# Modulation steps of a two-layer diffusion backbone, placed by hand around its layer norms

## The chip, the core and the metric

The kernel runs on one core of one Trainium2 chip. Its engines are TensorE (PE for the matmul, PEld for its weight load), VectorE (DVE), ScalarE (ACT), GpSimd (POOL) and SyncE (SP), which here only issues DMA transfers. The metric is the device time of one execution in microseconds; lower is better.

## The reference, cut to what matters

Two layers work on 384 tokens of width 1024: 128 context tokens (tile 0) and 256 latent tokens (tiles 1 and 2). A small matrix product on two conditioning vectors, `c_ctx` and `c`, gives each layer its six modulation vectors (shift, scale and gate, for each of the two sub-layers):

```python
mod = silu(c) @ ada_w[l] + ada_b[l]                    # ada_w[l] is 1024 x 6144
shift1, scale1, gate1, shift2, scale2, gate2 = split(mod, 6)
mix = mixing_sublayer(x * (1 + scale1) + shift1)       # mLSTM, convolution, retention, merged by gates
x = layer_norm(ALPHA * x + gate1 * mix, ln1_w, ln1_b)
h = x * (1 + scale2) + shift2
a, gt = split(h @ ffn_w13, 2)                          # 1024 x 5632
x = layer_norm(ALPHA * x + gate2 * ((silu(gt) * a) @ ffn_w2), ln2_w, ln2_b)
```

All is float32. The outputs are the tokens and the final states of the context's scans.

## The kernel before, in words

**Matmuls.** A float32 product is made of three fast ones: activations and weights are each split into a high and a low part (`whl`, `split`, L205 on ACT and L206 on DVE), and `accum` (L255 to L257) adds high x high, high x low and low x high in PSUM. `colsA` makes channel-major results, all 384 tokens at a time; `tokB` makes token-major ones, one tile of 128 tokens and 512 channels at a time, which is 24 matmuls for a depth of 1024. `wrows` and `wcols` load weights in pieces of up to 1 MB into three buffers (wraw, L211 and L243), all issued from SP's queue.

**Modulation steps.** A layer's modulation is cut into three blocks of 2048 columns. `ada_steps` (L356) turns one block into nine closures: eight each load 1 MB of `ada_w` into wada (L369; one buffer, `WADA = 1`) and run four short matmuls into one PSUM bank (L371; eight records each); the first also loads the bias, the eighth adds it on DVE (L375) and sends the gates out through POOL's queue (L381); the ninth transposes the rows (L387) and copies them to `modT`. Layer 0's first block is computed ahead of everything. The other five, 45 closures, lie in the list `fillers`; `fill()` (L153) runs the next one. They have due times: the norm after layer 0's mixing needs the first two blocks, the norm after its FFN the third, and the loops at L1077 and L1097 run what is missing by then.

**Where they run.** `tick()` (L161) is called after each group of matmuls. It adds `rate["fill"]`, 0.3, to a counter, and at each whole number it runs one step. So there is a step behind every third or fourth group, wherever that falls, until the list is empty.

**The norms.** `proj` (L453) multiplies by an output weight in two halves of 512 channels, three token tiles each, and adds the gated result to the residual x (`resid`, L423 to L431). In the last half `norm` follows per tile: the statistics on DVE (L436, L318), the power -0.5 on POOL (L319), the normalisation on DVE (L442). Then `after(t)` runs `make_hT`: eight transposes of x on PE (L306), scale and shift on ACT (L310), the split into high and low on DVE (L313, L314), so that h2 (or h1 of the next layer) is there for the next projection; and `affine` on POOL (L450, L451), which brings x itself up to date. `after` is held back by one tile: tile 0's transposes come behind tile 1's matmuls, tile 1's behind tile 2's, and tile 2's in the middle of the second tile of the next projection (`lead`, the parameter `mid` of `tokB`). The next projection is `ffn_in` (L887; its first 512 columns go by `tokB`) after the mixing, and the value projections of layer 1 (L1110 to L1114) after layer 0's FFN. After layer 1's FFN comes the output; there is no `after`.

**Order.** The kernel is written in the Tile framework. The framework puts each engine's instructions in order by its own model of when each is ready, with the program's order as the priority; so an engine's order can differ from the program's.

Of the kernel before, what the change touches and what calls it, by code (L numbers as in the profile page):

```python
# [35 lines left out]
WADA = 1  # L36
TAPS1, TAPS2 = 2.0, 4.5
FILL = 0.3
LEADN = 4
AORD = {(0, 0): ((1, 1, 0, 16),), (0, 1): ((0, 1),), (0, 4): ((1, 2, 0, 16),), (0, 5): ((0, 2),),  # L40
        (1, 3): ((1, 3, 0, 16),), (1, 5): ((0, 3),)}
# [4 lines left out]
O_MQ, O_MK, O_MV, O_MO, O_MG = 0, 512, 1024, 1536, 2048  # L46
# [51 lines left out]
def tile_kernel(ctx: ExitStack, tc: tile.TileContext, a: dict, o: list):  # L98
# [17 lines left out]
    def psum(name="ps"):  # L116
        return pp.tile([P, 512], F32, tag="ps", name=name)
# [4 lines left out]
    def tmp(shape, tag, bufs=2, dt=F32):  # L122
        n = 1
        for v in shape[1:]:
            n *= v
        if n in NB and bufs != 1:
            return sm.tile(list(shape), dt, tag=f"w{n}", name=tag, bufs=NB[n])
        return sm.tile(list(shape), dt, tag=tag, name=tag, bufs=bufs)
# [7 lines left out]
    rate = {"fill": 0.0, "acc": 0.0, "taps": 0.0, "tacc": 0.0}  # L136
# [16 lines left out]
    def fill(n=1):  # L153
        for _ in range(min(n, len(fillers))):
            fillers.pop(0)()
# [68 lines left out]
    def wrows(src, nk):  # L224

        out = []
        for k0 in range(0, nk, 4):
            n = min(4, nk - k0)
            raw = wraw(src[k0 * P:(k0 + n) * P, :], n)
            for k in range(0, n, 2):  # L230
                hi, lo = whl([P, 2, 512], raw[:, k:k + 2, :])
                out += [(hi[:, i, :], lo[:, i, :]) for i in range(2)]
        return out
# [17 lines left out]
    def accum(out, pairs, first=True, last=True):  # L251

        n = len(pairs)
        for i, ((sh, sl), (vh, vl)) in enumerate(pairs):
            mm(out, sh, vh, start=(first and i == 0), stop=False)  # L255
            mm(out, sh, vl, start=False, stop=False)  # L256
            mm(out, sl, vh, start=False, stop=(last and i == n - 1))  # L257
# [27 lines left out]
    def tokB(ha, w, t, mid=None):  # L285

        ps = psum()
        s = slice(t * P, (t + 1) * P)
        pairs = [(ha.part(k, s), w[k]) for k in range(len(w))]
        if mid is None:  # L290
            accum(ps, pairs)
        else:
            n = len(w) * LEADN // 8
            accum(ps, pairs[:n], True, False)
            mid()
            accum(ps, pairs[n:], False, True)
        return ps
# [96 lines left out]
    def mod_affine(shift, scale, w, b):  # L394

        S = tmp((P, KT, 2), "modS")
        ts_(S, scale, 1.0, None, op0=ALU.add)
        B = tmp((P, KT, 2), "modB")
        for m in range(2):
            tt(B[:, :, m], S[:, :, m], b, op=ALU.mult)  # L400
            tt(B[:, :, m], B[:, :, m], shift[:, :, m], op=ALU.add)
            tt(S[:, :, m], S[:, :, m], w, op=ALU.mult)
        return S, B
# [49 lines left out]
    def proj(src, w, lc, first, final=False, after=None):  # L453


        nk = w.shape[0] // P
        late = []
        for hf in range(2):
            wl = wrows(w[:, hf * 512:(hf + 1) * 512], nk)
            for t in range(NT):  # L460
                ps = tokB(src, wl, t)
                resid(t, hf, ps, lc, first, final)
                if final and hf == 1:
                    norm(t, lc if after is None else None)
                    if after is None:
                        put_out(t)
                    else:
                        late.append(t)
                        if len(late) > 1:
                            after(late.pop(0))  # L470
                tick()
        return lambda: [after(t) for t in late]

    def put_out(t):
        for hf in range(2):
            s = slice(hf * 512, (hf + 1) * 512)
            if t == 0:
                nc.sync.dma_start(y_prompt[0, :, s], x[0][:, s])
            else:
                nc.sync.dma_start(y_sample[0, (t - 1) * P:t * P, s], x[t][:, s])  # L480

    def pv(l, v, n):
        return pvec[:, l, v:v + n]


    def put_v(dst, e):
        return lambda ps, t: nc.scalar.copy(dst[:, t, :, 0:e], ps.rearrange("p (h e) -> p h e", e=e))

    def alloc_v():
        v1 = sm.tile([P, NT, NH, 129], F32, tag="v1", name="v1", bufs=1)  # L490
        nc.gpsimd.memset(v1[:, :, :, 128:129], 1.0)
        return v1
# [394 lines left out]
    def ffn_in(l, h2, k0, n, lead=None):  # L887

        fA = Act(n, "fA")
        w = a["ffn_w13"][l]  # L890
        c0 = k0 * P
        if lead is not None:
            sgB = []
            wl = wrows(w[:, FF + c0:FF + c0 + 512], KT)
            for t in range(NT):
                ps = tokB(h2, wl, t, lead if t == NT - 2 else None)
                s_ = tmp((P, 512), "sgB")
                act(s_, ps, AF.Silu)
                sgB.append(s_)
                tick()  # L900
            wl = wrows(w[:, c0:c0 + 512], KT)

            def turn(t):
                ps = psum()
                for j in range(4):
                    tr(ps[:, j * P:(j + 1) * P], sgB[t][:, j * P:(j + 1) * P], ident)  # L906
                fA.put4(0, t, ps.rearrange("p (j c) -> p j c", c=P))

            for t in range(NT):
                ps = tokB(h2, wl, t)  # L910
                tt(sgB[t], ps, sgB[t], op=ALU.mult)
                if t:
                    turn(t - 1)
                tick()
            late = [lambda: turn(NT - 1)]
            c0 += 512
        else:
            late = []
        for c1 in range(c0, (k0 + n) * P, 256):
            sg = {}  # L920

            def put_g(ps, j):
                sg[j] = tmp((P, T), "sig")
                act(sg[j], ps, AF.Silu)

            def put_a(ps, j):
                f = tmp((P, T), "gf")
                tt(f, ps, sg[j], op=ALU.mult)  # L928
                fA.put(j, f)

            colsA(w[:, FF + c1:FF + c1 + 256], 256, h2, KT, put_g, c1 // P - k0)
            for f in late:
                f()
            late = []
            colsA(w[:, c1:c1 + 256], 256, h2, KT, put_a, c1 // P - k0)
        return fA
# [136 lines left out]
    fillers += ada_steps(0, 1) + ada_steps(0, 2) + ada_steps(1, 0) + ada_steps(1, 1) + ada_steps(1, 2)  # L1073
    rate["fill"] = FILL
    for l in range(DEPTH):
        mA = mixing(l, ha, v1, rv)
        while l == 0 and len(fillers) > 27:  # L1077
            fill()
        S2, B2 = mod_affine(modT[l][:, 1, 8:16, :], modT[l][:, 2, 0:8, :], pv(l, V_L1W, 8), pv(l, V_L1B, 8))
        h2 = Act(KT, "h2")  # L1080
        lc = ln_consts(l, 0)

        def after1(t):
            make_hT(h2, t, S2, B2)
            affine(t, lc)

        lead = proj(mA, a["out_w"][l], lc, True, True, after1)
        lc2 = None
        for k0, n in ((0, 8), (8, 6), (14, 8)):
            fA = ffn_in(l, h2, k0, n, lead if k0 == 0 else None)  # L1090
            if lc2 is None:
                lc2 = ln_consts(l, 1)
            w2 = a["ffn_w2"][l, k0 * P:(k0 + n) * P, :]
            if k0 + n < KF:
                proj(fA, w2, lc2, k0 == 0)
            elif l + 1 < DEPTH:
                while len(fillers) > 18:  # L1097
                    fill()
                S1, B1 = mod_affine(modT[l + 1][:, 0, 0:8, :], modT[l + 1][:, 0, 8:16, :],
                                    pv(l, V_L2W, 8), pv(l, V_L2B, 8))  # L1100
                ha = Act(KT, "h1")

                def after2(t):
                    make_hT(ha, t, S1, B1)
                    affine(t, lc2)

                lead2 = proj(fA, w2, lc2, False, True, after2)
                v1 = alloc_v()
                rv = m6((P, NT, NH, P), name="rv")
                for off, dst in ((O_MV, v1), (O_RV, rv)):  # L1110
                    wl = wrows(a["in_w"][l + 1][:, off:off + 512], KT)
                    for t in range(NT):
                        put_v(dst, P)(tokB(ha, wl, t, lead2 if t == NT - 2 and off == O_MV else None), t)
                        tick()  # L1114
            else:
                proj(fA, w2, lc2, False, True)
# [28 lines left out]
```

## Time and profile before

| | |
|---|---|
| median of 3 runs | 1488.73 us (1486.75 to 1489.26) |
| profiled execution, its own time | 1490.92 us |
| its span | 1488.9 us |
| mean granted clock of PE | 0.984 of full speed |
| HBM read | 221.18 MB |

A page of the profile tells what each engine did in one execution. "Busy" is time in which an instruction ran. PE's matmuls overlap, so their durations add up to more than the time they take; the distance between starts is what one costs. In a timeline each row has the start in us from the start of the span, the length in us, the engine, the line of the kernel, the operation, result <- inputs, shape, count, and in brackets the engine's idle time before it with what ended it. Names are the program's: ps and adaps are PSUM banks, whi and wlo the halves of a weight, h1h, h1l, h2h and h2l those of an activation.

### The profile page before, as it was taken

The numbers are of one execution on the slowest core, as the hardware profiler recorded it, in microseconds if no ns is written. First come the engines' busy times: TensorE is split into PE (matmuls) and PEld (weight loads), VectorE is DVE, ScalarE is ACT, GpSimd is POOL, SyncE is SP. The second block draws the span as 40 slices with busy tenths as digits, with TensorE's granted clock in tenths as the row PEclk, the third lists the DMA queues.
The fourth block names the chain that finished last, engine by engine and source line by source line (L and its number), as shares of the span: only waits on it lengthen the run. The fifth ranks groups of instructions, "written<-read, shape, count | busy, mean of one in ns | idle before, by whom it ended". The sixth has DMA issues, their size and how long they took to land. (4 is left out here: it accounts for less than half of the span.)

```text
span 1488.9 us, 20492 instructions
## 1 busy us (share of the span) xinstructions
PE 1438.7 (97%) x7990; PEld 1302.5 (87%) x7990; DVE 944.7 (63%) x1755; ACT 576.8 (39%) x1026; POOL 233.2 (16%) x242
## 2 busy tenths in 40 slices
PE   6999999999998999999999999989999989999997
PEld 4799999989986888979967999989999869899996
DVE  3457688996647545354375477989975674454446
ACT  2434555332523423323243345553325243242330
POOL 1003233002214100000042023320021250000000
PEclk8999999999999999999999999999999999999999
DMA  9465352464473474645644532324434525243441
GB/s 330 159 226 173 125 185 87 154 226 158 138 259 128 142 254 131 222 155 173 212 141 122 162 118 81 118 68 124 132 108 147 169 71 202 82 155 100 142 156 42
DMA packets 131713, 226.22 MB, mean 152 GB/s; under 512 B 12552, under 2 KB 62200, under 8 KB 126496
## 3 DMA queue, kind: packets, MB, share of 16 engines
q1 hardware_dynamic: 130144, 222.78, 45.2%
q0 software_dynamic: 1472, 2.14, 0.5%
q8 instruction: 62, 1.02, 0.3%
q14 instruction: 35, 0.29, 0.1%
HBM read 221.18 MB, written 3.71 MB: 151 GB/s over the span
## 5 line engine op out<-in xcount | busy, mean ns | idle before, releaser
L205 ACT CAST whi<-wraw 128x512 fp32r<-128x512 f32 (+1 forms) x484 | 338.7, 722 | 624.5 <-PE ps L256 268.1
L206 DVE TENSOR_TENSOR wlo<-wraw,whi 128x512 fp32r<-128x512 f32 (+1 forms) x484 | 403.5, 857 | 195.4 <-PE ps L257 92.4
L255 PE MATMUL ps<-h1h,whi 128*128 128x384 f32 x896 | 306.0, 341 | 0.0
L257 PE MATMUL ps<-h1h,wlo 128*128 128x384 f32 x896 | 299.9, 335 | 0.0
L256 PE MATMUL ps<-h1l,whi 128*128 128x384 f32 x896 | 299.8, 335 | 0.0
L255 PE MATMUL ps<-h2h,whi 128*128 128x384 f32 x576 | 193.9, 337 | 0.0
L257 PE MATMUL ps<-h2h,wlo 128*128 128x384 f32 x576 | 192.6, 334 | 0.0
L256 PE MATMUL ps<-h2l,whi 128*128 128x384 f32 x576 | 192.6, 334 | 0.0
L255 PEld LDWEIGHTS ps<-h1h,whi 128*128 128x128 f32 x896 | 168.4, 188 | 13.7 <-issue 8.4
L256 PEld LDWEIGHTS ps<-h1l,whi 128*128 128x128 f32 x896 | 168.5, 188 | 0.1
L257 PEld LDWEIGHTS ps<-h1h,wlo 128*128 128x128 f32 x896 | 168.3, 188 | 0.0
L756 DVE SCALAR_TENSOR_TENSOR cacc<-u,cwt,cacc 128x399 f32<-128x399 f32 x232 | 148.6, 661 | 2.0
L255 PEld LDWEIGHTS ps<-h2h,whi 128*128 128x128 f32 x576 | 108.1, 188 | 8.5 <-issue 4.2
L256 PEld LDWEIGHTS ps<-h2l,whi 128*128 128x128 f32 x576 | 108.1, 188 | 0.2
L257 PEld LDWEIGHTS ps<-h2h,wlo 128*128 128x128 f32 x576 | 108.1, 188 | 0.0
L255 PE MATMUL ps<-whi,fAh 128*128 128x512 f32 x264 | 103.4, 392 | 0.0
L257 PE MATMUL ps<-whi,fAl 128*128 128x512 f32 x264 | 102.9, 390 | 0.0
L256 PE MATMUL ps<-wlo,fAh 128*128 128x512 f32 x264 | 102.8, 389 | 0.0
L423 DVE TENSOR_TENSOR gmix<-ps,lnc 128x512 f32<-128x512 f32 x48 | 33.1, 689 | 81.2 <-PE ps L257 81.2
L928 DVE TENSOR_TENSOR gf<-ps,sig 128x384 f32<-128x384 f32 x36 | 20.1, 558 | 91.1 <-PE ps L257 91.1
L319 POOL TENSOR_TENSOR rs<-rs_ve,half 128x1 f32<-128x1 f32 x18 | 15.4, 856 | 380.8 <-DVE rs_ve L318 380.8
L844 POOL TENSOR_TENSOR mg<-mg,sig 128x384 f32<-128x384 f32 x32 | 42.4, 1330 | 200.5 <-DVE sig L843 200.5
(303 smaller groups left out, 2194.8 us busy)
## 6 DMA issues: line engine op xcount, KB each, us to landing
wraw<-in_in_w_dram SPq DMA_DIRECT2D x64, 1024.0 KB
wada<-in_ada_w_dram SPq DMA_DIRECT2D x40, 1024.0 KB
wraw<-in_ffn_w_dram SPq DMA_DIRECT2D x76, 512.0 KB
wraw<-in_ffn_w_dram SPq DMA_DIRECT2D x28, 1024.0 KB
wraw<-in_out_w_dram SPq DMA_DIRECT2D x8, 1024.0 KB
adaq<-in_ada_w_dram SPq DMA_DIRECT2D x8, 512.0 KB
wraw<-in_mlstm_out_w_dram SPq DMA_DIRECT2D x4, 1024.0 KB
wraw<-in_ret_out_w_dram SPq DMA_DIRECT2D x4, 1024.0 KB
```

The lines of the kernel that those rows point to most:

```text
L205: nc.scalar.copy(hi, src)
L206: tt(lo, src, hi.bitcast(F32), op=ALU.subtract)
L255: mm(out, sh, vh, start=(first and i == 0), stop=False)
L256: mm(out, sh, vl, start=False, stop=False)
L257: mm(out, sl, vh, start=False, stop=(last and i == n - 1))
L319: nc.gpsimd.tensor_tensor(out, ve, half[:, 0:shape[1]], op=ALU.pow)
L423: tt(g, ps, lc[0 if t == 0 else 1, hf], op=ALU.mult)
L756: stt(ac, u[:, k:k + CW], wk, ac, op0=ALU.mult, op1=ALU.add)
L844: nc.gpsimd.tensor_tensor(dst, dst, sg[j], op=ALU.add)
L928: tt(f, ps, sg[j], op=ALU.mult)
```

## The change

Three places get a call of `fill()`: in `proj`, ahead of each `after(t)` (the one that is left for later is now a function that fills first); in `ffn_in`, ahead of the second token tile of the first projection; and ahead of the second token tile of layer 1's first value projection. The rate of the counter is lowered from 0.3 to 0.1 from the end of layer 0's mixing until the end of its FFN, and to 0.0 in layer 1's; between them 0.3 holds again.

```diff
+FILLS = (0.1, 0.0)
...
                     else:
                         late.append(t)
                         if len(late) > 1:
+                            fill()
                             after(late.pop(0))
                 tick()
-        return lambda: [after(t) for t in late]
+        def rest():
+            fill()
+            for t in late:
+                after(t)
+
+        return rest
...
             for t in range(NT):
+                if t == 1:
+                    fill()
                 ps = tokB(h2, wl, t, lead if t == NT - 2 else None)
...
             fill()
+        rate["fill"] = FILLS[l]
         S2, B2 = mod_affine(modT[l][:, 1, 8:16, :], modT[l][:, 2, 0:8, :], pv(l, V_L1W, 8), pv(l, V_L1B, 8))
...
                 lead2 = proj(fA, w2, lc2, False, True, after2)
+                rate["fill"] = FILL
                 v1 = alloc_v()
                 rv = m6((P, NT, NH, P), name="rv")
                 for off, dst in ((O_MV, v1), (O_RV, rv)):
                     wl = wrows(a["in_w"][l + 1][:, off:off + 512], KT)
                     for t in range(NT):
+                        if t == 1 and off == O_MV:
+                            fill()
                         put_v(dst, P)(tokB(ha, wl, t, lead2 if t == NT - 2 and off == O_MV else None), t)
                         tick()
```

## Rows read from the trace of the kernel before

**Rows 1.** The page, part 1: busy time, share of the span, instructions.
```profile
PE 1438.7 (97%) x7990; PEld 1302.5 (87%) x7990; DVE 944.7 (63%) x1755; ACT 576.8 (39%) x1026; POOL 233.2 (16%) x242
```

**Rows 2.** PE's timeline, first norm: start, length, instruction, idle before.
```profile
458.90 1.03 PE L306 MATMUL ps<-cc,x 128*128 128x128 f32 x8
...
459.87 1.07 PE L371 MATMUL adaps<-wada,cs 128*32 128x512 f32 x8
...
467.83 1.11 PE L306 MATMUL ps<-cc,x 128*128 128x128 f32 x8 [1.22 <-DVE x L442]
...
476.83 0.50 PE L255 MATMUL ps<-whi,h2h 128*128 128x512 f32 x1 [1.68 <-DVE h2h L313]
...
478.52 0.80 PE L257 MATMUL ps<-whi,h2l 128*128 128x512 f32 x1 [0.95 <-DVE h2l L314]
...
482.95 1.85 PE L306 MATMUL ps<-cc,x 128*128 128x128 f32 x8
...
487.50 1.06 PE L371 MATMUL adaps<-wada,cs 128*32 128x512 f32 x8
...
488.49 0.50 PE L255 MATMUL ps<-whi,h2h 128*128 128x512 f32 x1
```

**Rows 3.** Windows: busy time by engine, granted clock, DMA share, GB/s.
```profile
465.00:466.00 1.00, 1.00 (x7) 0.81 (x5) 1.00 (x1) 0.68 (x2) 1.00 (x2) 1.00 0.20 82
...
784.00:786.00 2.00, 2.00 (x6) 1.52 (x5) 1.56 (x5) 0.00 (x0) 0.99 (x1) 0.50 0.62 185
```

**Rows 4.** POOL's timeline, first norm.
```profile
459.58 2.98 POOL L450 TENSOR_TENSOR x<-x,lnc 128x512 f32<-128x512 f32 x2 [2.65 <-PE ps L306]
...
465.67 1.53 POOL L319 TENSOR_TENSOR rs<-rs_ve,half 128x1 f32<-128x1 f32 x1
```

**Rows 5.** PE's timeline, second norm and first norm of layer 1.
```profile
773.03 1.11 PE L306 MATMUL ps<-cc,x 128*128 128x128 f32 x8 [1.22 <-DVE x L442]
...
782.02 0.79 PE L255 MATMUL ps<-whi,h1h 128*128 128x512 f32 x1 [1.67 <-DVE h1h L313]
...
1188.72 1.03 PE L306 MATMUL ps<-cc,x 128*128 128x128 f32 x8
...
1197.64 1.67 PE L306 MATMUL ps<-cc,x 128*128 128x128 f32 x8 [2.40 <-DVE x L442]
```

**Rows 6.** PE's timeline, both ends of the FFN body of layers 0 and 1.
```profile
504.96 0.60 PE L906 MATMUL ps<-cc,sgB 128*128 128x128 f32 x4
...
735.62 0.39 PE L255 MATMUL ps<-whi,fAh 128*128 128x512 f32 x1
...
1233.99 0.60 PE L906 MATMUL ps<-cc,sgB 128*128 128x128 f32 x4
...
1447.85 0.39 PE L255 MATMUL ps<-whi,fAh 128*128 128x512 f32 x1
```

**Rows 7.** DVE's timeline, first norm.
```profile
464.55 2.24 DVE L206 TENSOR_TENSOR wlo<-wraw,whi 128x1024 fp32r<-128x1024 f32 x1
...
486.94 1.65 DVE L314 TENSOR_TENSOR h2l<-hf,h2h 128x512 fp32r<-128x512 f32 x1
```

**Rows 8.** Instructions that touch tile x: durations ns min/median/max, first, last.
```profile
L425 DVE SCALAR_TENSOR_TENSOR x<-x,gmix x24: 691/693/1774, 436.8 to 1308.2; 128x512 f32<-128x512 f32 x24
```

**Rows 9.** SP's timeline: DMA issues, three stretches.
```profile
294.43 0.97 SPq L243 DMA_DIRECT2D wraw<-in_in_w_dram  x2
...
296.87 0.34 SPq L369 DMA_DIRECT2D wada<-in_ada_w_dram  x1
...
461.00 0.34 SPq L369 DMA_DIRECT2D wada<-in_ada_w_dram  x1
...
774.93 0.37 SPq L211 DMA_DIRECT2D wraw<-in_in_w_dram  x1
...
778.89 0.37 SPq L243 DMA_DIRECT2D wraw<-in_in_w_dram  x1
```

**Rows 10.** PE's timeline, a step in layer 0's branches.
```profile
309.68 1.15 PE L371 MATMUL adaps<-wada,cs 128*32 128x512 f32 x8 [2.24 <-DMA wada<-in_ada_w_dram]
```

## The prediction

> **What bounds the kernel now.** I read the page's busy times first: PE is busy for 1438.7 us, 97% of the span [rows 1]. A PE step that is moved from one full stretch to another therefore changes nothing; it gains only where PE would have stood still. So I looked next at where PE stands still, in PE's timeline around the first norm of layer 0, line 1087 [rows 2]. The reader is to see three sets of transposes (L306, one per token tile: 458.90, 467.83, 482.95) and waits behind them: 1.22 us before the second set, then 1.68 and 0.95 us in the first half of the second token tile of the next projection. From 478.52 on the clock is low too: that matmul takes 0.80 us, the transposes at 482.95 take 1.85 instead of 1.03, and in the windows view the same place of the second norm, 784 to 786, has a granted clock of 0.50, so 1.2 GHz instead of 2.4 [rows 3].
>
> Then I asked who makes PE wait, in POOL's timeline [rows 4]. The first transposes release POOL's affine work on that tile (459.58); it lasts until 465.67, where POOL takes the next tile's L319 at once, and only behind that can DVE normalise (L442) and PE transpose. From transposes to transposes that is 467.83 - 458.90 = 8.93 us. In layer 1, where no step stands between, it is 1197.64 - 1188.72 = 8.92 us [rows 5]. The norm's chain sets this distance, not PE's work. The second norm of layer 0 has nearly the same waits, 1.22 and 1.67 us [rows 5].
>
> **The change, part by part.** *What moves.* There are 45 steps (40 with a 1 MB wada load and short matmuls, 5 that close a block), before and after. Following the counter in `tick` through the code: up to line 1087 nothing changes. In the FFN body of layer 0 (first L906 to the last projection) 15 steps become 5; in layer 1's mixing 3 become 8. Between the first transposes and the third tile of the next projection there were 2 steps in each of layer 0's two norms; now there are 4: one ahead of each set of transposes, one ahead of the second tile. One stays ahead of each stretch, in another place, and one more comes after the second. In layer 1's norms nothing is left to run, so `FILLS[1]` and the calls do nothing there.
>
> *What a step costs in a full stretch.* Layer 0's FFN body, with 15 steps, takes 735.62 - 504.96 = 230.66 us; layer 1's, without any, 1447.85 - 1233.99 = 213.86 [rows 6]. So 16.8 / 15 = 1.12 us each, and one step on PE's timeline is 1.07 us [rows 2]. Four steps leave full stretches: 4 x 1.12 = -4.5 us. The five that go to layer 1's mixing I cost like any other, nothing hides them: no gain, no loss.
>
> *What they cost in the norm.* I walk the first norm with old times from [rows 2] and a step of 1.07. The step that stood behind the first transposes now stands ahead: they start at 459.97, and the projection's third tile where it did. The second transposes can come at 467.83 (the chain isn't delayed) or at 459.97 + 8.93 = 468.90. I take the latter, because 8.92 and 8.93 agree without and with a step behind; the new step ahead of them is then hidden by a wait of 1.22 + 1.07. The next projection's first tile ended at 476.83 - 1.68 = 475.15, now 1.07 later, at 476.22. The step ahead of the second tile ends at 477.29, and that tile's h2 comes at 476.83 + 1.07 = 477.90: the wait of 1.68 shrinks to 0.6 and this step is hidden too. The matmul that waited until 478.52 starts at 479.59. The remaining ten matmuls of the half tile took 482.95 - 478.52 = 4.43 us at the low clock; at the high one twelve took 487.50 - 484.80 = 2.70, so I estimate 2.4 for ten behind a wait. With the fourth step the third transposes come at 483.05, against 482.95. DVE finished their first h2l at 486.94 + 1.65 = 488.59, 5.64 us behind them [rows 7]; with transposes at the high clock some 0.5 us earlier. The tile's third matmul needs it, 0.6 us in. So the third tile can run as if it had started at 487.6, against 488.49: **-0.9 us** if the clock holds. If it falls as now, the transposes come 2.1 us later and the tile at 490.2: **+1.7 us**. Both ends serve for the second norm too.
>
> Which? The clock is low after waits of 1.68 + 0.95 us in one norm, after 1.67 in the other, and after a single 2.40 in layer 1, where the transposes take 1.67; it is high after 1.22 [rows 2, 5]. The new waits are about 1.2, 0.6 and 0.95, so I count on one norm with the high clock and one with the low: -0.9 + 1.7 = +0.8 us.
>
> DVE works beside POOL here: L425, with two inputs in SBUF, takes 0.69 us as a rule and up to 1.77 [rows 8]. The Trainium skill (SBUF — State Buffer, Who interferes with whom) says that a VectorE instruction with two SBUF inputs contends with a GpSimd instruction that reads SBUF, and that issue order decides who waits. By it L425 would now be through before the later affine work, which could hand back 1.77 - 0.69 = 1.1 us per norm and make the sum 2.2 us lower; the rows have POOL's own queue as the last link before L442, so this stands outside the sum.
>
> *DMA and SP.* wada has one buffer: a step's load starts when the step before has run. With nothing else in flight a load issued at 461.00 is down by 465.2 [rows 9], when its traffic ends (82 GB/s in the slice from 465 on) [rows 3]. The closest steps are the third and fourth: 477.29 to some 482.0, 4.7 us, enough in the first norm. On SP a wada load waits for PE with weight loads behind it; those of the next projection were issued before the first transposes, so I cost this at nothing; without that cover it is the second rival below. In the second norm the loads in flight are in_w's: issued at 774.93 and 778.89 [rows 9], they still move 185 GB/s at 784 to 786 [rows 3]. A wada load behind two of in_w's, issued at 296.87, let PE stand for 2.24 us until 309.68 [rows 9, 10]: 12.8 us. So the fourth step there waits between 0 and 12.8 - 4.7 = 8.1 us, with the third transposes queued behind it on PE. Its load is issued at about 783, on average 6.1 us after in_w's two; in that row it was 2.4. That is 3.7 us further on, so I estimate 8.1 - 3.7 = 4.4 us. But instruction order here is the framework's, not the program's: DVE runs a weight split of the next projection at 464.55 in the middle of a norm [rows 7]. Transposes placed ahead of a step that isn't ready lose nothing. I take the mean of both orders, 2.2 us.
>
> *Sum:* -4.5 + 0.8 + 2.2 = **-1.5 us**. The profiled execution took 1490.92 us (span 1488.9), 2.2 us more than the median of 1488.73; all terms are differences, so I set them against the median: **1487.2 us**. A measurement can tell about 0.2% from no change, 3.0 us here.
>
> **The rivals.** *Both norms keep the high clock and no load is late:* -4.5 - 1.8 = -6.3 us, 1482.4 us. For it: the steps fill just the waits after which the clock falls. Against: the delayed chain, by which three waits are left, and a clock that fell after no more than 1.67 us.
>
> *Slower, the single wada buffer:* in the second norm the fourth step waits 4.4 us and the first about 1 us (its load meets in_w's as well), while both clocks fall: -4.5 + 3.4 + 5.4 = +4.3 us, 1493.0 us. It decides when the waits for wada pass 4.1 us, which is what the steps gain with both clocks low and the 3.0 us of the measurement. For it: until now the steps stood far apart, and even so one load was late by 2.24 [rows 10]. Against: in the first norm nothing is in flight. The Trainium skill (DMA: Bandwidth & Descriptors, Queues, rings and completion order) says that each DMA engine consumes one issuer's descriptors in ring order. By it wada gets nothing until SP's earlier loads are through, which speaks against this change; the 12.8 us agree.
>
> *The change doesn't do what it says:* the framework, finding a step's load not ready, places steps back among the matmuls behind the transposes, about as now. Then there is no difference, 1488.7 us. DVE's order shows that it can reorder; the steps themselves stand so far where the program has them.
>
> **How the numbers follow.** Forecast 0.42, high clock in both 0.31, late loads 0.18, order as now 0.09. The forecast's own range, -4 to +1 us, is nearly all within 0.2%; 0.05 of it lies beyond on the fast side and 0.01 on the slow. Faster: 0.31 + 0.05 = 0.36. Slower: 0.18 + 0.01 = 0.19. Same: 0.36 + 0.09 = 0.45. The range takes in the fast rival and the slow one, 1482 to 1493.5; beyond lie waits near the bound of 8 us, or the port's 2.2 us on top of the fast rival.
>
> **What would show it.** In the profile after: L371 at each of the four places in both norms; transposes still 8.9 us apart; waits before L306 and L255 about 1.1 us shorter; 5 steps in the FFN body, which is 11 us shorter, and 5 more in layer 1's mixing. The second norm's L371 shows whether wada is waited for. I am wrong if the transposes move closer together (POOL was not the link), if L371 waits in the first norm too, or if the FFN body shrinks by much less than 1.1 us a step.

## The result, and the profile after

The changed kernel takes **1497.89 us** (median of 4 executions, 1496.85 to 1499.57) against 1488.79: a ratio of 1.0062 [1.005, 1.0074], 9.1 us slower. Timed once more beside the kernel before it took 1498.39 against 1488.98, 1.0057 [1.0043, 1.0071].

The page's first part shows PE a little less busy in a longer span, where [rows 1] had 1438.7 us and 97%:

```profile
PE 1437.4 (96%) x7990; PEld 1299.3 (87%) x7990; DVE 939.7 (63%) x1755; ACT 574.8 (38%) x1026; POOL 226.8 (15%) x242
```

So the loss is idle time. To find its place I cut both spans at the same instructions and asked for the windows between: layer 0's output projection up to the first transposes, from there to the first L906 (after: L915), the FFN body, the last FFN projection up to the second norm's transposes, from there to layer 1's first gate matmul, layer 1's mixing, and layer 1's first norm. Columns: window, length, then busy us (instructions) of PE, PEld, DVE, ACT, POOL, granted clock, DMA share, GB/s. Before:

```profile
428.87:458.90 30.03, 29.16 (x129) 22.32 (x129) 18.03 (x26) 6.20 (x7) 3.47 (x3) 1.00 0.58 200
458.90:504.96 46.06, 41.78 (x185) 31.69 (x184) 31.32 (x35) 20.41 (x37) 23.61 (x14) 0.93 0.31 103
504.96:735.62 230.66, 230.66 (x1265) 205.40 (x1264) 105.42 (x163) 76.13 (x126) 3.08 (x6) 1.00 0.56 194
735.62:764.10 28.48, 28.48 (x130) 22.57 (x130) 16.66 (x23) 5.70 (x6) 0.56 (x1) 1.00 0.49 148
764.10:816.49 52.39, 48.60 (x218) 35.51 (x216) 36.57 (x42) 24.50 (x46) 24.60 (x15) 0.93 0.41 121
816.49:1159.88 343.39, 335.79 (x2016) 329.35 (x2012) 264.11 (x568) 154.90 (x289) 69.39 (x79) 0.99 0.39 120
1159.88:1233.99 74.11, 67.71 (x289) 53.59 (x289) 48.80 (x61) 26.27 (x44) 26.27 (x17) 0.95 0.29 98
```

After:

```profile
429.90:461.06 31.16, 30.27 (x138) 22.34 (x137) 18.45 (x28) 6.20 (x7) 3.47 (x3) 1.00 0.55 194
461.06:508.63 47.57, 42.55 (x196) 30.80 (x193) 29.39 (x34) 20.05 (x37) 19.44 (x14) 0.93 0.42 144
508.63:727.74 219.11, 219.11 (x1189) 203.69 (x1188) 104.29 (x161) 75.81 (x126) 0.53 (x1) 1.00 0.47 161
727.74:760.79 33.05, 30.39 (x137) 22.58 (x137) 18.63 (x28) 5.68 (x6) 0.55 (x1) 0.98 0.43 127
760.79:816.83 56.04, 50.63 (x233) 36.49 (x229) 31.61 (x39) 24.26 (x46) 25.19 (x20) 0.92 0.50 151
816.83:1167.65 350.82, 341.84 (x2056) 328.93 (x2053) 263.65 (x568) 153.94 (x289) 69.80 (x79) 1.00 0.42 133
1167.65:1240.46 72.81, 66.39 (x290) 52.42 (x290) 48.80 (x61) 26.26 (x44) 26.41 (x17) 0.98 0.30 100
```

The body gives back 11.55 us. The first norm (windows 1 and 2) costs 2.64, the second (4 and 5) 8.22, layer 1's mixing 7.43; what lies outside these differs by -0.2 (1.0 more ahead of them, 1.3 less in layer 1's first norm). That is the 6.5 us between the two spans. The executions as a whole lie further apart: 86 of the kernel before, timed through the study, have a mean span of 1487.3 us, against 1488.9 in the profile; ten of the changed kernel have 1495.8, against 1495.4. So the profile of before was a long one, and the stages, which give 6.5 of 8.5 us, don't show where its 2 us lie.

PE's timeline in the first norm answers to [rows 2]. The first row is still of the kernel before, the others are of the changed one:

```profile
473.73 0.50 PE L256 MATMUL ps<-wlo,h2h 128*128 128x512 f32 x1 [0.43 <-DVE wlo L206]
...
460.06 1.06 PE L372 MATMUL adaps<-wada,cs 128*32 128x512 f32 x8
461.06 1.09 PE L307 MATMUL ps<-cc,x 128*128 128x128 f32 x8
...
467.53 1.06 PE L372 MATMUL adaps<-wada,cs 128*32 128x512 f32 x8
468.53 1.09 PE L307 MATMUL ps<-cc,x 128*128 128x128 f32 x8
...
474.95 0.50 PE L257 MATMUL ps<-wlo,h2h 128*128 128x512 f32 x1 [2.22 <-DVE wlo L207]
...
478.37 0.80 PE L257 MATMUL ps<-wlo,h2h 128*128 128x512 f32 x1 [1.23 <-DVE wlo L207]
...
484.65 1.07 PE L372 MATMUL adaps<-wada,cs 128*32 128x512 f32 x8
...
487.37 1.03 PE L307 MATMUL ps<-cc,x 128*128 128x128 f32 x8
...
490.87 1.07 PE L372 MATMUL adaps<-wada,cs 128*32 128x512 f32 x8
```

The reader is to see that the wait of 1.22 us ahead of the second transposes is gone, as was forecast, and that others are there in its place: PE now waits for wlo, the low halves of the next projection's weights, which before cost it 0.43. The fourth step isn't where the program has it: the framework put it behind the third transposes, here (490.87) and in the second norm (792.27). In the second norm, answering to [rows 5], the first step waits for its own load, and the clock is low behind it; later PE waits for wlo again, 1.17 and 2.78 us (the last row is of SP; it holds two issues, the first at 750.76):

```profile
749.63 1.07 PE L372 MATMUL adaps<-wada,cs 128*32 128x512 f32 x8
759.03 1.83 PE L372 MATMUL adaps<-wada,cs 128*32 128x512 f32 x8 [2.66 <-DMA wada<-in_ada_w_dram]
760.79 1.96 PE L307 MATMUL ps<-cc,x 128*128 128x128 f32 x8
...
774.72 0.50 PE L257 MATMUL ps<-wlo,h1h 128*128 128x512 f32 x1 [1.17 <-DVE wlo L207]
...
781.09 0.79 PE L257 MATMUL ps<-wlo,h1h 128*128 128x512 f32 x1 [2.78 <-DVE wlo L207]
...
750.76 10.48 SPq L370 DMA_DIRECT2D wada<-in_ada_w_dram  x2
```

### The profile page after: what moved, and what is told of

Same layout as the page of the kernel before. It is cut to its first block, busy times and chain, and to the rows that moved or that the text cites. A ratio compares the mean times of both kernels' runs of the same rounds, so it can differ in the third digit from the quotient of the medians.

```text
span 1495.4 us, 20494 instructions
## 1 busy us (share of the span) xinstructions
PE 1437.4 (96%) x7990; PEld 1299.3 (87%) x7990; DVE 939.7 (63%) x1755; ACT 574.8 (38%) x1026; POOL 226.8 (15%) x242
## 5 line engine op out<-in xcount | busy, mean ns | idle before, releaser
L320 POOL TENSOR_TENSOR rs<-rs_ve,half 128x1 f32<-128x1 f32 x18 | 14.4, 798 | 502.1 <-DVE rs_ve L319 502.1
```

Of the source, the lines that this page charges most:

```text
L320: nc.gpsimd.tensor_tensor(out, ve, half[:, 0:shape[1]], op=ALU.pow)
```

## The experiments

For every kernel: the median, the ratio to the kernel before beside it with its 95% interval, and from its profile the length of the four stretches with the steps in them (in brackets, from PE's instruction stream). One profile's norm stretch varies by 1 to 3 us with the clock, the mixing by about 3.

| kernel | us | ratio | first norm | body | second norm | mixing |
|---|---|---|---|---|---|---|
| before | 1488.79 | | 76.09 (3) | 230.66 (15) | 80.87 (4) | 343.39 (3) |
| after | 1497.89 | 1.0062 [1.005, 1.0074] | 78.73 (5) | 219.11 (5) | 89.09 (7) | 350.82 (8) |
| e1_rate_only | 1498.86 | 1.006 [1.0044, 1.0076] | 74.70 (1) | 220.25 (6) | 81.42 (3) | 362.91 (15) |
| e2_fills_only | 1497.17 | 1.005 [1.0033, 1.0067] | 80.52 (7) | 231.44 (15) | 82.14 (3) | 342.42 (0) |
| e3_no_first | 1498.84 | 1.0053 [1.0034, 1.0072] | 78.59 (4) | 219.10 (5) | 85.53 (6) | 353.92 (10) |
| e5_t1_only | 1496.74 | 1.0049 [1.0034, 1.0064] | 74.97 (2) | 219.11 (5) | 82.91 (4) | 362.18 (14) |
| e6_before_one_load | 1486.73 | 0.9982 [0.9973, 0.9992] | 73.31 (3) | 230.68 (15) | 80.28 (4) | 343.71 (3) |
| e7_after_one_load | 1494.66 | 1.0035 [1.002, 1.005] | 81.14 (5) | 219.15 (5) | 86.60 (7) | 351.74 (8) |
| e8_shift | 1494.78 | 1.0036 [1.0023, 1.005] | 78.96 (4) | 230.56 (15) | 82.13 (3) | 343.94 (3) |
| e9_before_t1 | 1487.09 | 0.9981 [0.9971, 0.9991] | 74.98 (4) | 230.63 (15) | 80.27 (4) | 342.21 (2) |
| e10_piece4_late | 1490.95 | 1.0015 [1.0003, 1.0027] | 76.51 (3) | 230.68 (15) | 81.50 (4) | 344.96 (3) |
| e11_after_wfirst | 1493.64 | 1.003 [1.0016, 1.0044] | 76.92 (5) | 219.16 (5) | 88.18 (7) | 350.82 (8) |
| e12_t1_wfirst | 1481.28 | 0.995 [0.9936, 0.9965] | 72.49 (4) | 230.63 (15) | 77.75 (4) | 342.25 (2) |
| e13_before_wfirst | 1483.41 | 0.9962 [0.995, 0.9973] | 72.50 (3) | 230.68 (15) | 79.23 (4) | 343.76 (3) |
| e14_calls_wfirst | 1493.66 | 1.003 [1.0013, 1.0047] | 79.42 (7) | 231.44 (15) | 81.22 (3) | 341.06 (0) |
| e15_rate_wfirst | 1491.68 | 1.002 [1.0009, 1.0031] | 72.50 (1) | 220.25 (6) | 79.10 (3) | 361.71 (15) |
| e19_t1t1_wfirst | 1485.03 | 0.9977 [0.9967, 0.9987] | 72.41 (4) | 230.64 (15) | 82.46 (5) | 341.71 (1) |

### The change in parts

e1 has the new rates and no new call, e2 the new calls and the old rate, e3 all but the step ahead of tile 0's transposes, e5 only the step ahead of the second token tile.

```diff
-FILLS = (0.1, 0.0)
+FILLS = (0.3, 0.3)
```

```diff
-                            fill()
+                            if late[0]:
+                                fill()
                             after(late.pop(0))
```

(The first is e2, the second e3; e1 and e5 only take out `fill()` lines.)

> The changed kernel without its new calls ahead of the transposes and of the second tiles; the lower rate alone is left. Five steps stay in layer 0's FFN body as in the changed kernel, no step is left between the first transposes and the third tile in either norm, and 15 steps (3 before, 8 in the changed kernel) fall into layer 1's mixing. Order theory (a step ahead of the first transposes makes the framework put the norm of tile 1 ahead of tile 0's splits on DVE, and DVE then stands waiting for POOL) and late-load theory (PE waits for wada in the second norm): both norms run without those waits; at 1.12 us a step wherever it stands the time is 1488.8, within 2 us. Mixing theory (a step costs 1.49 us there: 350.82 - 343.39 over 5): 12 steps more at 0.37 extra, 1493, and the mixing takes 361 instead of 357 us.

> The changed kernel with the rate left at 0.3 throughout: all new calls, FFN body as before the change, no step at all in layer 1's mixing. In the norms a called step and one of the counter now stand right behind each other, so the load of the second starts when it should run. Late-load theory: a step waits about 4.2 us for its load at two or three places in each norm, slower than the changed kernel by 5 us or more, 1503 or above. Order theory alone: the same DVE order in the first norm as in the changed kernel and the same loss, 1496 to 1498. Mixing theory alone: no steps there, 3 x 1.49 saved against the kernel before, 1486 to 1489.

> The changed kernel without the step ahead of the first token tile's transposes in both norms; the three other places stay, 10 steps in the mixing instead of 8. Order theory: DVE takes tile 0's h2 ahead of tile 1's normalisation again, its idle time of 3.39 us there is gone and the stretch from the first transposes to the first L915 is 2 us shorter than the 47.57 of the changed kernel. Late-load theory: the wait of 2.66 us ahead of the second norm's first transposes is gone, and with it the low clock behind it. Both together 1491 to 1493; order alone 1495, late loads alone 1494. Mixing theory alone: 1498 to 1499.

> The changed kernel with the step ahead of the second token tile alone (one in each norm), none ahead of transposes; 14 steps in the mixing. If a step is hidden by the wait for that tile's h2 (1.68 and 1.67 us before the change), the time is 2 us less than with the rate alone. Order and late-load theory: 1487 to 1489. Mixing theory: 11 steps more than before the change at 0.37 extra, 1491 to 1493.

None comes back to the kernel before, 1489.29 us beside them: +9.6, +7.9, +9.6 and +7.5 us. Either half of the change is enough for nearly the whole loss, so the two losses don't add up: the new calls take steps out of the mixing that the rate alone would leave there. No theory has all four times: e2 lies in the range of the order theory (1496 to 1498), e3 in that of the mixing theory (1498 to 1499), e1 and e5 above every range. What the rate costs can be read in e1: the body gives 10.4 us for nine steps, layer 1's mixing takes 19.5 for twelve. In that mixing the steps outrun their loads (waits in e1's mixing: total us, times, longest):

```profile
PE adaps L372 <- DMA wada<-in_ada_w_dram: 7.5, 2, 6.6
```

And the first norm in e5 against e1: one more step, 0.3 us more, so that step looks hidden; the difference is within what the clock does to such a stretch, and e12 against e13 below repeats it. In e3 against e5 two steps more, those written ahead of the second and third tiles' transposes: 3.6 us more in the first norm and 2.6 in the second, so those are not.

The order theory had one thing right. In the first norm of the changed kernel DVE takes the second tile's statistics ahead of the first tile's splits and then stands idle for POOL:

```profile
466.13 1.97 DVE L443 TENSOR_SCALAR x<-x,mv,rs 128x512 f32<-128x512 f32 x2 [3.39 <-POOL rs L320]
```

In e1, e3 and e5, without the call ahead of the first transposes, that idle time is 0.44 us, as before the change. Yet e3's first norm is no shorter for it (78.59 against 78.73): there PE waits 2.55 us for the last piece of wlo instead.

### Late loads against everything else

e6 and e7 are the kernels before and after with seven of eight wada loads left out.

```diff
-                wt = wp.tile([P, 2048], F32, tag="wada", name="wada", bufs=WADA)
-                nc.sync.dma_start(wt, a["ada_w"][l, k * P:(k + 1) * P, b * 2048:(b + 1) * 2048])
+                if k == 0:
+                    st["wt"] = wp.tile([P, 2048], F32, tag="wada", name="wada", bufs=WADA)
+                    nc.sync.dma_start(st["wt"], a["ada_w"][l, 0:P, b * 2048:(b + 1) * 2048])
+                wt = st["wt"]
```

> The kernel before, with the weight tile of a modulation block loaded at the block's first step only and used by its other seven steps too: seven of eight of the 1 MB loads are left out, and the modulation comes out of the wrong rows; the steps, their number and their places stay. It is the base for the changed kernel without these loads. Theory A (the changed kernel loses because its steps come closer together than their loads): little or nothing here, 1484 to 1489, since no step of the kernel before waits for its tile from the first norm on. Theory B (the loads take bandwidth and queue time from other loads even where no step waits): 1475 to 1483.

> The changed kernel with the same loads left out (one load for each block of eight steps). Theory A (late loads): the 2.7 us wait ahead of the second norm's first transposes goes, with the low clock behind it, and the distance to the same cut of the kernel before falls from 9 to 3 us or less. Theory B (the steps cost their 1.1 us wherever they stand, in the norms too, and the order of DVE's work that comes with them costs the rest): the distance stays 6 us or more.

The distance between the two is 7.9 us, where it was 9.1. The wait of 2.66 us goes, with the low clock behind it: up to the second norm's first transposes e7 takes 1.09 us more than e6 (29.56 against 28.47), one step, where after against before it was 4.57. Most of the loss stays, so theory A falls. PE's waits for wlo stay too, 2.7 and 3.0 us in e7's two norms.

### Only the places

e8 adds nothing but half a step to the counter once, behind layer 0's mixing.

```diff
+        if l == 0:
+            rate["acc"] += 0.5
```

> The kernel before, with half a step added to the counter once, behind layer 0's mixing: every later step comes one or two groups of products earlier; no step goes to another stretch but one from layer 1's mixing to the FFN body. Theory C (the places of the kernel before happen to suit, and any other set of places loses): 1494 or more. Theory D (it is what the change does, the steps taken out of the FFN body and put ahead of transposes, that costs): within 2 us of the kernel before, 1487 to 1491.

> The kernel before with one call added: the step between the first and the second token tile of the projection behind the norm; the rates are as before. The one call that cost only 0.3 us in its stretch when it was tried with the new rates. If that step is hidden by itself and the rate is what loses: 1486 to 1490, same as before. If every change of the places loses (theory C): 1494 or more.

e8 is 5.1 us slower, with the body as long as before. Its first norm has one step more and takes 2.9 us more, its second one step less and takes 1.3 more (the expectation had no step change places there). PE's waits behind the first transposes:

```profile
PE ps L256 <- DVE wlo L206: 3.2, 2, 2.5
PE ps L306 <- DVE x L442: 2.4, 1, 2.4
PE ps L257 <- DVE h2l L314: 0.9, 1, 0.9
PE ps L255 <- DVE h2h L313: 0.5, 1, 0.5
```

This is the key reading: PE waits for wlo in e8 as in the changed kernel, without any new call. It isn't the same piece each time. Each token tile needs four pieces of wlo in turn. In e8's two norms the long wait is for the fourth (2.55 us in both), as in the changed kernel's second norm (2.78 of 3.95 us). In the changed kernel's first norm it is for the second (2.22 of 3.83), behind the 3.39 us in which DVE stands for POOL. The instruction streams show where the fourth comes from. These are the results of DVE's instructions from the second tile's statistics to the third tile's normalisation (e10 a little further), in each kernel's order. x1 and x2 are tiles 1 and 2; x2 stands for the residual sum first and for the normalisation at the end. e10 and e13 come up below:

```
before  bn h2h mv h2l rs_ve wlo x1 h2h wlo h2l wlo gmix wlo x2 h2h bn h2l mv h2h rs_ve h2l x2
e8      bn h2h mv wlo rs_ve h2l x1 h2h wlo h2l gmix wlo x2 h2h bn h2l mv h2h rs_ve wlo x2
after   bn mv rs_ve x1 h2h wlo h2l h2h wlo h2l gmix wlo x2 h2h bn h2l mv h2h rs_ve wlo x2
e13     bn h2h mv h2l rs_ve wlo x1 h2h wlo h2l wlo wlo gmix x2 bn h2h mv h2l rs_ve h2h x2
e10     bn h2h mv h2l rs_ve wlo x1 h2h wlo h2l wlo gmix x2 bn h2h mv h2l rs_ve h2h x2 h2l wlo
```

The framework orders each engine by when it believes instructions to be ready. With the steps elsewhere on PE, DVE's order is another: in the kernel before, all four wlo pieces stand ahead of the third tile's residual sum; after the change and after the mere shift the fourth stands behind its rs_ve. e9 keeps the rates and DVE's order of before, adds the one step that looked hidden in e5, and is 2.6 us faster.

### Is it the fourth piece?

e10 takes the kernel before and holds the fourth piece back behind rs_ve (a forced order on DVE, no wait); e11, e12 and e13 write the next projection's weights into the program ahead of the third tile's residual sum, in the changed kernel, in e9 and in the kernel before. They do so in every norm with a projection behind it, layer 1's first one too.

```diff
...
+                    with tc.issue_after(tail):
+                        hi, lo = whl([P, 2, 512], raw[:, k:k + 2, :])
...
```

```diff
                 ps = tokB(src, wl, t)
+                if ahead is not None and hf == 1 and t == NT - 1:
+                    early.append(ahead())
                 resid(t, hf, ps, lc, first, final)
```

> The kernel before, all steps at their places; only in layer 0's two norms the fourth piece of the next projection's weights is split on DVE behind the third token tile's rs_ve, as DVE's order has it in the changed kernel and in the shifted one, in place of ahead of that tile's residual sum. Theory E (the steps' places tip the order of DVE's instructions, and the late fourth piece is what PE then waits for): waits for wlo of 2 to 3 us in each of the two norms, and 1492 to 1496. Theory F (the order on DVE only moves the same idle time about): 1487 to 1491.

> The changed kernel with the next projection's weights written into the program ahead of the third token tile's residual sum, so that all four pieces are split before that tile's norm. Theory E: the long wait for wlo goes from both norms of layer 0, and the time falls by 2 to 5 us, to 1493 to 1496. Theory F: 1496 to 1499, as changed.

> The kernel before with the one call between the first and second token tile (1487.1 alone) and the weights written ahead as well. Its fourth piece was early already, so theory E expects little: 1485 to 1488. It is also the candidate for the fastest kernel of the study.

> The kernel before with the weights written ahead alone: the control for the two above. Theory E and theory F alike: 1487 to 1491, no difference that can be measured; if it is faster by more than 2 us, the earlier fourth piece is worth something in the kernel before too.

Delaying the piece makes PE wait 1.7 and 2.5 us for it in the two norms and costs 2.2 us, less than the 3 us or more that theory E expected and within theory F's range; writing it ahead brings the changed kernel 4.3 us (across two timings) and, against both theories, the kernel before 5.4. Some of these two gains isn't layer 0's. In layer 1's first norm, where no step is left, the kernel before itself has the order of e8, with the fourth piece behind rs_ve (PE waits only 0.4 us for wlo there); with the weights ahead that norm takes 71.2 to 71.3 us in every profile, without them 72.8 to 75.0.

e10 isn't the kernel before with one piece moved: the rest of DVE's order changed with it, into that of e13 (the last two streams above). So the better comparison is e10 against e13. ACT and POOL have one order in both, and DVE's in layer 0's norms differs by the place of the one piece:

```profile
457.67:504.11 46.44, 41.28 (x186) 30.89 (x185) 31.02 (x35) 20.40 (x37) 22.77 (x14) 0.93 0.32 102
...
459.41:501.80 42.39, 38.92 (x186) 29.38 (x185) 31.15 (x35) 20.38 (x37) 24.04 (x14) 1.00 0.34 112
```

Timed side by side they are 7.5 us apart (1490.95 and 1483.41): 4.0 us in the first norm, part of it the clock, 2.3 in the second and 1.5 in layer 1's first, where e10 keeps the order of before. In this order the late piece costs some 6 us (an estimate, 7.5 - 1.5), so theory E holds there. It isn't the whole of the changed kernel: e11 keeps a wait of 2.20 us for the second piece in its first norm, and in its second, where the waits for wlo are gone, another step waits 3.14 us for its load.

Where the order is good even the old places gain. In e12 the windows row of the first norm behind the transposes, and PE's waits in it:

```profile
459.63:502.01 42.38, 39.90 (x194) 29.53 (x192) 31.14 (x35) 20.39 (x37) 24.03 (x14) 1.00 0.42 137
...
PE ps L307 <- DVE x L444: 1.2, 1, 1.2
PE ps L258 <- DVE rs_ve L319: 0.9, 1, 0.9
PE ps L256 <- DVE h2h L314: 0.3, 1, 0.3
```

42.38 us with three steps, against 46.06 and 44.80 with two in the two profiles of before: no wait for wlo, and the clock holds. e13 takes 42.39 with two, so the third is hidden in full. **e12 is the fastest kernel, 1481.28 us, 0.995 [0.9936, 0.9965]**, below the 1485 to 1488 that was expected of it.

### What is left with the weights ahead

> All new calls of the change, with the rate of the kernel before (0.3 throughout) and the weights written ahead: to be held against the kernel before with the weights ahead (1483.4). Theory G (with the order on DVE mended, the calls ahead of the transposes are harmless and the lowered rate is what loses): 1481 to 1485. Theory H (a step ahead of transposes costs its full 1.1 us and more, wherever the weights are written): 1487 to 1491, with 1 to 4 us more in each of the stretches of layer 0's norms.

> The lowered rate alone (0.1, then 0.3 and 0 as in the change), no new call, with the weights written ahead: to be held against 1483.4 as well. Theory G (the twelve steps that the lower rate puts into layer 1's mixing run ahead of their loads there): 1489 to 1494, with waits for wada of 5 us and more in that mixing. Theory H (the rate is harmless once the norms are mended): 1481 to 1485.

Against 1483.4 (separate timings, each beside the kernel before) the calls cost 10.3 us and the rate 8.3, both together (e11) 10.2. Theory G holds for the rate. For the calls theory H holds in sign; the time is above its 1487 to 1491. e15's norms are no longer than e13's, and its mixing takes 18.0 us more for twelve steps, with 7.7 us of waits for wada. e14's first norm takes 6.9 us more with four more steps; part of it is that a block closes there (2.1 us of waiting for mrows) and that steps outrun loads (1.8). In its second norm PE still waits 3.95 us for the second piece of wlo, so writing the weights ahead doesn't mend every order.

### The same programs again

> The kernel before, unchanged, profiled a second time: how far one profiled execution of it stands from another. If the low clock in its two norm stretches (0.93 both, 46.06 and 52.39 us) belongs to the program, it is there again within 0.3 us; if it comes and goes from run to run, a stretch at a clock near 1.00 takes some 2 to 3 us less.

> The changed kernel, unchanged, profiled a second time. Its waits should be where they were: one of 2 to 3 us for wada at the second norm's first step and 3 to 4 us for wlo in each of layer 0's norms; the granted clock of the norm stretches may differ from the first profile's 0.93 and 0.92.

> The changed kernel, unchanged, timed in five rounds beside the kernel before. The account by stages, from two profiled executions of each, gives 5 us (single pairs up to 7); the first timing gave 9.1. If the account is complete: 1493 to 1496 here. If something that the stages don't show is missing: 1497 to 1499 again.

The kernel before took 1494.84 us in this execution, above all its timed ones; its norms were shorter (74.87 and 80.29), its mixing longer (346.31). The changed kernel took 1496.38, then 1498.39 in the median; its three profiles agree on the norms (78.73, 79.20, 78.41 and 89.09, 88.78, 88.85), so the loss there belongs to the program. The clock in the norm of before does not: the same stretch, with the same order and, within 0.1 us, the same waits of 1.7, 1.2, 1.0 and 0.4, in the repeat and in e6:

```profile
462.06:506.86 44.80, 40.58 (x186) 30.53 (x184) 31.24 (x35) 20.39 (x37) 23.57 (x14) 0.96 0.34 106
...
456.14:499.38 43.24, 38.99 (x185) 29.38 (x184) 31.26 (x35) 20.40 (x37) 23.58 (x14) 1.00 0.19 61
```

46.06, 44.80 and 43.24 us at 0.93, 0.96 and 1.00.

With 1498.39 us the account by stages is not complete, by the expectation's own terms: some 2 us between the kernels lie where these profiles don't show them.

### One step more behind the second norm

> The fastest kernel so far (weights written ahead, one step between the first token tiles behind the first norm, 1481.3) with the same call behind the second norm too. If such a step is hidden there as well (1.1 us less in layer 1's mixing): 1479.5 to 1481.5. If it comes ahead of its load, which follows the step before it: 1482 to 1486, with a wait for wada in that stretch.

1485.03, slower than e12 by 3.7 us. The next step, 13 us later, waits for its load, 3.77 us, and then takes 1.94 us at the low clock instead of 1.07. That is 4.6 of the 4.7 us by which the second norm is longer than e12's, so the added step itself is hidden.

```profile
776.48 1.07 PE L372 MATMUL adaps<-wada,cs 128*32 128x512 f32 x8
...
789.60 1.94 PE L372 MATMUL adaps<-wada,cs 128*32 128x512 f32 x8 [3.77 <-DMA wada<-in_ada_w_dram]
```

## Why the prediction was wrong

**A step in the FFN body, 1.12 us: right.** Ten fewer gave 11.55 us, 1.16 each. The counts, 15 to 5 and 3 to 8, came out as well.

**The five in layer 1's mixing "like any other": mis-sized.** Forecast 5.6 us, measured 7.4 in the profiled pair. Over all kernels with the loads the mixing takes 341 to 342 us with none to two steps, 343 to 346 with three, 350 to 353 with eight, 362 to 363 with fourteen or fifteen: about 1.3 us each from three to eight and 1.6 from eight to fifteen, where steps wait for wada. In the changed kernel's mixing no step waits for its load: PE is busy for 6.05 us more, 1.2 a step, and idle for 1.4 us more. Why eight steps cost more than 1.07 each wasn't tried by itself.

**Hidden steps in the norms: the step that failed.** I walked the norm with the old times and held the other engines' order fixed, though I had seen the framework put a weight split into a norm. The waits I filled did shrink; DVE's new order then made PE wait 3.8 and 4.0 us for wlo. The forecast had the first norm at -0.9 or +1.7 and it cost 2.64. With late loads and the step behind the second norm it had 4.1 us for both norms (0.8 + 2.2 + 1.1), and they cost 10.9; five more steps at 1.12 are 5.6 of that, as if none were hidden. Order alone is worth a good part of it: with the weights ahead and the steps as they were, the first norm is 1.8 us shorter in e11 and 3.6 in e13, in single profiles. Of the four calls only the one ahead of the second token tile is hidden (e5, e12); those ahead of the transposes cost their full time or more (e3 against e5; 1.13 us for the first, in a window where PE is busy for 29.16 of 30.03 us). The rival "order as now" was right in part: the fourth step stands behind the third transposes in both norms. In the walk, twelve matmuls at the high clock took 487.50 - 484.51 = 2.99 us, not 2.70, which is too little to matter.

**The fixed distance between the transposes: wrong**, by the sign I had named: they are 468.53 - 461.06 = 7.47 us apart, not 8.93. POOL is still the last link (DVE stands 3.39 us for its rs ahead of L443), but its order isn't the old one. With DVE's statistics ahead of its splits, POOL takes L320 between the halves of its affine work instead of behind it:

```profile
464.30 1.29 POOL L452 TENSOR_TENSOR x<-x,lnc 128x512 f32<-128x512 f32 x1
465.55 0.55 POOL L320 TENSOR_TENSOR rs<-rs_ve,half 128x1 f32<-128x1 f32 x1
466.06 1.30 POOL L452 TENSOR_TENSOR x<-x,lnc 128x512 f32<-128x512 f32 x1
```

**The late load: right place, wrong step.** I gave the second norm's fourth step 2.2 us. It was the first that waited, 2.66 us, 9.4 us behind the step before it, and with the low clock this made 3.5 us up to the transposes. The fourth, moved behind them, didn't wait here; in the two repeats the first waits 2.51 and 2.44, and a later step 1.44 and 1.77. The rival had the first at about 1 us. That rival's time (1493.0) was nearest, but its mechanism is the smaller part: without the loads 7.9 of 9.1 us stay.

On SP, which I had put at nothing, the load of the first norm's third step was issued at 475.40, behind a weight load and 6.9 us after the step before it had ended; no wait of PE for it shows.

**The clock.** I had counted on one norm at the high clock; behind the first transposes both fell short of it, in all three profiles (0.89 to 0.96 and 0.92 to 0.94). That it falls after 1.68 us and holds after 1.22 is no rule: behind the same waits it fell, fell less and held.

**The port.** The third tile's residual sum (L425, now L426) takes 0.68 us, not the 1.77 that it took beside POOL's L450, but not because it came ahead of POOL's later affine work: it runs behind it, at 478.24, while POOL is idle. The two durations agree with what the Trainium skill (SBUF — State Buffer, Who interferes with whom) says of two-input work beside GpSimd. Nothing was handed back, since other DVE work took its place beside POOL:

```profile
472.62 2.28 DVE L207 TENSOR_TENSOR wlo<-wraw,whi 128x1024 fp32r<-128x1024 f32 x1
...
477.10 1.21 DVE L207 TENSOR_TENSOR wlo<-wraw,whi 128x1024 fp32r<-128x1024 f32 x1
478.24 0.68 DVE L426 SCALAR_TENSOR_TENSOR x<-x,gmix 128x512 f32<-128x512 f32 x1
...
472.37 3.66 POOL L452 TENSOR_TENSOR x<-x,lnc 128x512 f32<-128x512 f32 x2
```

The same split takes 1.21 us alone and 2.28 beside L452, and it is the work PE then waits for.

**What stays open.** Why the order of before suits was read from the streams, and the fourth piece is only part of it. The idle time of DVE behind the early statistics wasn't taken out by itself with everything else in place, and how much the rest of DVE's order is worth, each place by itself, wasn't tried. The 9.1 us are not split into parts that add up.

## What to carry to other kernels

Where a framework orders the engines, independent work moved on one engine reorders the others: compare the instruction streams of both kernels before walking old times, and shift the same work by a tick as a control. A step fits into a wait only if nothing behind it waits for the same chain, and with one buffer each step needs the time of its load behind the one before. Here the cheapest gain was to write the next stage's weights into the program earlier.

## What the runs showed of the hardware that was not expected

The span of one program goes with the granted clock: executions of the kernel before at a mean clock of 0.991 have a mean span of 1485.2 us (8 of them), those at 0.985 1488.6 (9 of them). And slowing goes both ways between DVE and POOL: POOL's two L450 take 2.98 us in the first norm of before [rows 4] and twice that for the next tile, where DVE splits weights and activations beside them:

```profile
468.57 6.25 POOL L450 TENSOR_TENSOR x<-x,lnc 128x512 f32<-128x512 f32 x2 [1.38 <-DVE h2h L313]
```
